# The order of small products in an RWKV-7 stage: three yields, a split solver, and sixteen gate pieces in the first group

## The chip, the cores and the metric

The kernel runs on one core of a Trainium2 chip. A core has five engines that run on their own and meet only at semaphores: TensorE (PE, matrix products; its weight loads are the row PEld), VectorE (DVE), ScalarE (ACT), GpSimd (POOL) and SyncE (SP, which here issues most of the DMA transfers). The metric is the device time of one execution in microseconds (us), and smaller is better.

## The reference, cut to what matters

The program is one layer of an encoder with four sequence mixers that share one projection, gates on their outputs, and a feed-forward network. The part that changes is the RWKV-7 mixer. Each of 8 heads keeps a 64 by 64 state S per direction, forward and backward over 1024 positions:

```python
S_t = S_{t-1} diag(w_t) + (S_{t-1} a_t) b_t^T + v_t k_t^T ;  y_t = S_t r_t
```

The other work in this stage belongs to the gates, `gates = sigmoid(u @ W_gate)`, which need nothing of the mixer and so can be computed at any moment:

```python
gates = jnp.split(jax.nn.sigmoid(p_gate), N_BRANCH, axis=-1)
merged = gates[0] * (ys[0] @ w_branch[l, 0])
for n in range(1, N_BRANCH):
    merged = merged + gates[n] * (ys[n] @ w_branch[l, n])
```

## The kernel before, in words

**Units.** The recurrence is done in chunks of 64 positions. A unit is one pair of heads (j of 0 to 3) and one block of 256 positions in each direction (bt of 0 to 3): 16 units, each with 4 chunks per direction. A unit passes through three generators. `rw_first` prepares it: `rw_dir` builds the operands `rw_AR` and `rw_BK` from decays (a scan on DVE, exponentials on ACT, products on DVE and POOL), then for each direction d eight products at L914 make the 64 by 64 coupling blocks, which DVE masks at L922 (four masks per d). When d = 1 is masked, `rw_solve` inverts the 16 by 16 diagonal blocks: eight DMAs bring the blocks to DRAM (`dA`, L967), two bring them back (`rw_SB`, `rw_pr`), ACT transposes one half (L973), DVE does a substitution in some 22 instructions (L981 to L994), two DMAs write the inverses out (`dT`, L997) and one reads them back in another layout (`rw_R`, L1000). `rw_second` assembles 64 by 64 inverses (`rw_TF`) from these in four pieces of 32 by 32 products (L1021, L1028, L1041, L1049). `rw_chain` then walks the four chunk steps of the unit.

**A chunk step of the chain.** L1112 multiplies the state by the operands (8 small products, called the step's first product below); ACT copies the result to `rw_s`; L1122 applies `rw_TF`, which gives u; ACT copies u into `rw_uv` (L1125); L1129 and L1136 form the new state in PSUM (L1136 reads u); DVE scales it into `rw_mv` for the next step (L1142; after the fourth step into `rw_M`). The outputs y are products at L1086 and L1091.

**Groups.** The loop in `rwkv` overlaps three units: in group g it runs the chain of unit g-1, the second part of unit g and the first part of unit g+1. One group has four steps, st = 0 to 3, which are the four chunk steps of the chain. Group 0 has no chain yet. Between these small products stand pieces of the gate work: one piece is 6 products of 128 by 512 (L125 to L127), 8 pieces make one column block of gates, and 28 column blocks (224 pieces) are spread over the stage. `GATE1` pieces run ahead of the groups, `GATE0` pieces in group 0, and `rate` says how many a step gets afterwards.

**What sets the order.** In the groups PE runs in exactly the order in which the Python code issues its instructions (`manual_schedule`). The queues of the other engines are ordered by the framework's scheduler, which starts from the same order and puts what is marked `high_priority` (the chain's own products, copies and state updates) further ahead. Each engine then works off its queue in order. The gates' weights come through `w_raw` (DMA by SP), `w_hi` (ACT) and `w_lo` (POOL), and a finished column block leaves PSUM through `gt` (ACT).

Of the kernel before, what the change touches and what calls it, by code (L numbers as in the profile page):

```python
# [23 lines left out]
class K:  # L24
# [661 lines left out]
    def rw_setup(self, wp):  # L686
        nc, a = self.nc, self.a
        self.rw_mask = self.t(wp, [P, 2, P], "rwm")
        self.rw_lm = self.t(wp, [P, 2, 32], "rwlm")
        self.rw_ST = self.t(wp, [64, 272], "rw_ST")  # L690
        nc.sync.dma_start(out=self.rw_ST[:, :256], in_=a["k_eye16"].to_broadcast([64, 256]))
        for tl, nm in ((self.rw_mask, "k_rwm"), (self.rw_lm, "k_rwl")):
            nc.sync.dma_start(out=tl, in_=a[nm])
        W = P * self.NB
        self.rw_rst = self.t(wp, [P, W], "rwrs", dt=BF16)
        nc.gpsimd.memset(self.rw_rst, 1.0)
        nc.gpsimd.memset(self.rw_rst[:, ::64], 0.0)

        NC = 2 * self.NB
        self.rw_TFt = [self.t(wp, [P, 2, NC, 64], f"rw_TF{i}") for i in range(2)]  # L700
        for x in self.rw_TFt:
            nc.gpsimd.memset(x, 0.0)
        self.rw_turn = 0
        self.rw_M = {}

        z = self.rw_TFt[0].rearrange("p d m t -> p (d m t)")
        for i in range(2):
            nc.sync.dma_start(out=self.dT[i].rearrange("g v x s t -> (g v x s t)").rearrange("(p n) -> p n", p=P),
                              in_=z[:, :256])
# [184 lines left out]
    def rw_first(self, j, bt, lin, wp):  # L894


        nc = self.nc
        NT, NB = T // P, self.NB
        NC = 2 * NB
        n0 = [bt * NB, NT - NB - bt * NB]  # L900
        cb = self.t(wp, [P, 2, NC, P], "rw_cb", bufs=3)
        gc = self.t(wp, [P, 2, NC], "rw_gc", bufs=3)
        ops = [self.rw_dir(j, d, n0[d], lin[d], gc[:, d], wp) for d in range(2)]
        b = dict(j=j, bt=bt, n0=n0, ar=[o[0] for o in ops], bk=[o[1] for o in ops], gc=gc, cb=cb, i=self.rw_turn)
        self.rw_turn += 1
        yield b
        for d in range(2):
            ar, bk, _ = ops[d]
            hrs = [(slice(64 * h, 64 * h + 64), slice(64 - 64 * h, P - 64 * h)) for h in range(2)]

            pts = [self.ps([P, NC, P], self.pat()) for h in range(2)]
            for c in range(NC):
                for h, (hr, _) in enumerate(hrs):
                    nc.tensor.matmul(pts[h][:, c, :], lhsT=bk[hr, c, :, :], rhs=ar[hr, c, :, h, :], start=True, stop=True)  # L914
            for h, (hr, ho) in enumerate(hrs):
                pt = pts[h]
                for o, rows, x in ((cb[hr, d], hr, pt[hr]),
                                   (ar[ho, :, :, h, :], ho, pt[ho].rearrange("p c (x t) -> p c x t", x=2))):
                    m = self.rw_mask[rows, d]
                    if len(o.shape) == 4:  # L920
                        m = m.rearrange("p (x t) -> p x t", x=2)
                    nc.vector.tensor_tensor(o, x, m.unsqueeze(1).to_broadcast(list(o.shape)), op=MUL)  # L922
            if d == 1:
                self.rw_solve(b, wp)
            yield
        pt = self.ps([P, 2, NB, 2], self.pat())
        for d in range(2):
            for n in range(NB):
                nc.tensor.matmul(pt[:, d, n, :], lhsT=ops[d][2][:, P * n:P * n + P], rhs=self.rw_sel[:, j, :],
                                 start=True, stop=True)  # L930
        for d in range(2):
            nc.scalar.copy(self.rw_coef[:, d, n0[d]:n0[d] + NB, 2 * j:2 * j + 2], pt[:, d])
        yield

    def rw_btm(self, b, wp):
# [19 lines left out]
    def rw_solve(self, b, wp):  # L955


        nc = self.nc
        NC = 2 * self.NB
        cb = b["cb"]  # L960
        rs = lambda q: slice(32 * q, 32 * q + 32)

        turn = b["i"] % 2
        dA = self.dA[turn].rearrange("(g u) (s t) -> u s g t", u=8, t=16)
        for u in range(8):
            o = 16 * (u % 4)
            nc.sync.dma_start(out=dA[u], in_=cb[16 * u:16 * u + 16, :, :, o:o + 16].rearrange("p d c t -> p (d c) t"))  # L967
        SB = self.t(wp, [64, 272], "rw_SB")
        pr = self.t(wp, [64, 256], "rw_pr")
        S1 = pr[:, :256].rearrange("p (s t) -> p s t", t=16)  # L970
        nc.sync.dma_start(out=SB[0:32, :256], in_=self.dA[turn, 0:32])
        nc.sync.dma_start(out=S1[32:64].rearrange("p s t -> p (s t)"), in_=self.dA[turn, 32:64])
        nc.scalar.copy(SB[32:64, :256].rearrange("p (s t) -> p s t", t=16), S1[32:64].rearrange("p s t -> p t s"))  # L973
        ST = self.rw_ST

        def view(x, w, o, n):

            return x.rearrange("p (x w) -> p x w", w=w)[:, :, o:o + 16 * n].rearrange("p x (i c) -> p x i c",
                                                                                     c=16)[:, :, :, :n]
        G = self.t(wp, [64, 64], "rw_G")  # L980
        nc.vector.tensor_copy(out=view(ST, 34, 1, 1), in_=view(SB, 34, 1, 1))  # L981
        for n in (2, 4, 8):
            x = 8 // n
            bij, tii, tjj, xij = [view(y, 34 * n, o, n) for y, o in ((SB, n), (ST, 0), (ST, 17 * n), (ST, n))]
            g3 = G[:, :x * n * n].rearrange("p (x i j) -> p x i j", x=x, i=n)
            m = min(n, 4)
            p4 = pr[:, :x * m * n * n].rearrange("p (x i j k) -> p x i j k", x=x, i=m, j=n)
            for l, r, o in ((bij, tjj, g3), (tii, g3, xij)):
                for i in range(0, n, m):
                    for y in range(x):  # L990
                        nc.vector.tensor_tensor(p4[:, y], l[:, y, i:i + m].unsqueeze(2).to_broadcast([64, m, n, n]),
                                                r[:, y].rearrange("p k j -> p j k").unsqueeze(1).to_broadcast(
                                                    [64, m, n, n]), op=MUL)
                    nc.vector.tensor_reduce(o[:, :, i:i + m], p4, axis=AX.X, op=ADD)  # L994

        for x in range(2):
            nc.sync.dma_start(out=self.dT[turn, :, :, x, :, 16 * x:16 * x + 16].rearrange("g v s t -> (g v) s t"),  # L997
                              in_=ST[x::2, :256].rearrange("p (s t) -> p s t", t=16))
        R = b["R"] = self.t(wp, [P, 2, NC, 32], "rw_R", bufs=2)
        nc.sync.dma_start(out=R.rearrange("p d m t -> p (d m) t"), in_=self.dT[turn].rearrange("g v x s t -> (v x s) g t"))  # L1000
# [56 lines left out]
    def rw_chain(self, b, wp):  # L1057


        nc = self.nc  # L1060
# [44 lines left out]
        for st in range(NC):  # L1105
# [24 lines left out]
                                     tile_position=(64 * h, 64 * h))  # L1130
            if st:
                y(st - 1, 0)
            with prio():
                for d, c in enumerate(cs):
                    for h, hr, _ in halves:
                        nc.tensor.matmul(pm[hr, d, :], lhsT=b["btm"][:, d, c, hr], rhs=b["uv"][:, d, c, h, :], start=False,  # L1136
                                         stop=True, tile_position=(0, 64 * h), skip_group_check=True)
                for h, hr, _ in halves:
                    g = b["gc"][hr, 0, st:st + 1]
# [119 lines left out]
    def rwkv(self, dr, dG, es, extra):  # L1259
        nc = self.nc  # L1260
# [40 lines left out]
        prev = None  # L1301

        with self.tc.manual_schedule(engines={mybir.EngineType.PE}):
            for g in range(n + 1):
                chn = self.rw_chain(prev, wp) if prev is not None else iter(())
                sec = self.rw_second(cur, wp) if cur is not None else iter(())
                fst, nxt = iter(()), None
                for st in range(4):
                    next(chn, None)
                    if st == 2:  # L1310
                        next(sec, None)
                    elif st == 3:
                        next(sec, None)
                        next(fst, None)
                    if prev is not None:
                        pieces(1)
                    next(chn, None)
                    if st == 0:
                        if cur is not None:
                            self.rw_btm(cur, wp)  # L1320
                        if g + 1 < n:
                            fst = self.rw_first(*order[g + 1], lin, wp)
                            nxt = next(fst)
                    elif st < 3:
                        next(fst, None)
                    if st > 1:
                        next(sec, None)
                    if st == 3 and g + 2 < n:
                        lin = self.rw_lin(*order[g + 2], wp)
                    if prev is None:  # L1330
                        pieces(self.GATE0 // 4)
                    else:
                        credit += rate if g < n else rate + self.ENDF / 2
                        k = int(credit + 1e-6)
                        credit -= k
                        pieces(k)
                next(chn, None)
                prev, cur = cur, nxt
            for _ in self.filler:
# [1 line left out]
        self.WP, self.wact = 300, False  # L1341

    HP = 300
    GATE0 = 8
    GATE1 = 8
    VA = 2
    NG = 28
# [751 lines left out]
```

## Time and profile before

| | |
|---|---|
| median of 3 runs | 2783.84 us (2767.37 to 2787.01) |
| the profiled execution, its own time | 2781.43 us |
| its span in the profile | 2779.6 us |
| PE busy | 2554.3 us, 92% |
| DVE, ACT, POOL busy | 64%, 33%, 43% |
| mean granted TensorE clock | 0.96 of full speed |

The profile names instructions by engine, line and operands: `L1136 MATMUL ppc<-rw_uv,rw_btm` writes a PSUM tile from the two tiles behind the arrow. "Idle before" is the time an engine stood still ahead of an instruction, and the name behind `<-` is what ended it. The granted clock (PEclk) is 1.00 at 2.4 GHz and 0.50 at 1.2 GHz; a value between is a mean over a stretch that has both. Times inside the span are counted from its start.

### The profile page before, as it was taken

The numbers are of one execution on the slowest core, as the hardware profiler recorded it, in microseconds if no ns is written. First come the engines' busy times: TensorE is split into PE (matmuls) and PEld (weight loads), VectorE is DVE, ScalarE is ACT, GpSimd is POOL, SyncE is SP. The second block draws the span as 40 slices with busy tenths as digits, with TensorE's granted clock in tenths as the row PEclk, the third lists the DMA queues.
The fourth block names the chain that finished last, engine by engine and source line by source line (L and its number), as shares of the span: only waits on it lengthen the run. The fifth ranks groups of instructions, "written<-read, shape, count | busy, mean of one in ns | idle before, by whom it ended". The sixth has DMA issues, their size and how long they took to land. (4 is left out here: it accounts for less than half of the span.)

```text
span 2779.6 us, 47056 instructions
## 1 busy us (share of the span) xinstructions
PE 2554.3 (92%) x18625; PEld 2044.3 (74%) x18625; DVE 1786.4 (64%) x2868; ACT 911.0 (33%) x1649; POOL 1194.1 (43%) x1164
## 2 busy tenths in 40 slices
PE   5999878999998899889989999999998999999998
PEld 4777656777776677678777777788776788888887
DVE  7577765676566642665562676457469998896444
ACT  4355532333333332333232232111234444442002
POOL 3654452343344323732222344357555444435332
PEclk9999988999999999999999979999999999999999
DMA  6422342443344323411111444455542222225222
GB/s 212 130 69 65 97 136 69 116 112 102 97 113 104 95 72 112 118 45 43 40 39 32 138 133 152 167 182 168 173 122 96 84 79 88 72 72 193 87 80 76
DMA packets 402117, 290.25 MB, mean 104 GB/s; under 512 B 121258, under 2 KB 364248, under 8 KB 401896
## 3 DMA queue, kind: packets, MB, share of 16 engines
q1 hardware_dynamic: 362920, 247.85, 30.6%
q10 hardware_dynamic: 38976, 39.40, 4.3%
q8 instruction: 146, 2.39, 0.4%
q14 instruction: 75, 0.61, 0.1%
HBM read 223.40 MB, written 63.77 MB: 103 GB/s over the span
## 5 line engine op out<-in xcount | busy, mean ns | idle before, releaser
L119 POOL TENSOR_TENSOR w_lo<-w_raw,w_hi 128x512 fp32r<-128x512 f32 x284 | 397.1, 1399 | 741.7 <-DVE w_hi L118 276.4
L125 PE MATMUL pbig<-uh,w_hi 128*128 128x512 f32 x1208 | 505.6, 420 | 20.5 <-ACT w_hi L116 8.9
L127 PE MATMUL pbig<-uh,w_lo 128*128 128x512 f32 x1208 | 483.4, 402 | 5.0 <-POOL w_lo L119 4.8
L126 PE MATMUL pbig<-ul,w_hi 128*128 128x512 f32 x1184 | 475.8, 402 | 0.0
L125 PEld LDWEIGHTS pbig<-uh,w_hi 128*128 128x128 f32 x1208 | 234.9, 195 | 86.8 <-ACT gt L1224 15.8
L127 PEld LDWEIGHTS pbig<-uh,w_lo 128*128 128x128 f32 x1208 | 232.9, 193 | 61.0 <-POOL w_lo L119 9.2
L126 PEld LDWEIGHTS pbig<-ul,w_hi 128*128 128x128 f32 x1184 | 230.2, 194 | 42.0 <-issue 0.9
L118 DVE CAST w_hi<-w_raw 128x512 fp32r<-128x512 f32 x224 | 136.4, 610 | 147.1 <-PE pbig L126 72.2
L127 PE MATMUL ppc<-uh,w_lo 128*128 128x512 f32 x340 | 134.1, 397 | 1.5 <-POOL w_lo L119 1.1
L125 PE MATMUL ppc<-uh,w_hi 128*128 128x512 f32 x340 | 134.2, 399 | 1.2 <-DVE w_hi L118 1.2
L126 PE MATMUL ppc<-ul,w_hi 128*128 128x512 f32 x320 | 126.6, 396 | 0.0
L125 PE MATMUL ppa<-uh,w_hi 128*128 128x512 f32 x220 | 88.5, 402 | 5.6 <-DVE w_hi L118 5.6
L127 PE MATMUL ppa<-uh,w_lo 128*128 128x512 f32 x220 | 87.0, 396 | 0.8 <-POOL w_lo L119 0.8
L127 PE MATMUL ppy<-uh,w_lo 128*128 128x512 f32 x216 | 85.1, 394 | 1.4 <-POOL w_lo L119 1.1
L125 PE MATMUL ppy<-uh,w_hi 128*128 128x512 f32 x216 | 85.3, 395 | 0.1
L1824 ACT CAST w_hi<-s 128x512 fp32r<-128x512 f32 x84 | 52.0, 619 | 97.8 <-PE pbig L126 23.7
L126 PE MATMUL ppa<-ul,w_hi 128*128 128x512 f32 x208 | 82.9, 399 | 0.0
L126 PE MATMUL ppy<-ul,w_hi 128*128 128x512 f32 x208 | 81.8, 393 | 0.0
L125 PEld LDWEIGHTS ppc<-uh,w_hi 128*128 128x128 f32 x340 | 64.9, 191 | 16.4 <-DVE w_hi L118 2.1
L127 PEld LDWEIGHTS ppc<-uh,w_lo 128*128 128x128 f32 x340 | 64.7, 191 | 16.4 <-POOL w_lo L119 1.5
L1375 DVE SCALAR_TENSOR_TENSOR ada_acc<-ada_w,sc,ada_acc 128x256 f32<-128x256 f32 x112 | 73.9, 662 | 2.0
L1142 DVE TENSOR_TENSOR rw_mv<-ppc,rw_gc 64x128 f32<-64x128 f32 x96 | 27.7, 289 | 73.5 <-PE ppc L1136 71.5
(789 smaller groups left out, 6361.9 us busy)
## 6 DMA issues: line engine op xcount, KB each, us to landing
w_raw<-in_w_in_dram SPq DMA_DIRECT2D x172, 256.0 KB
ada_w<-in_ada_w_dram SPq DMA_DIRECT2D x24, 1024.0 KB
s_raw<-in_ffn_up_dram SPq DMA_DIRECT2D x84, 256.0 KB
dG<-gt ACTq DMA_DIRECT2D x64, 256.0 KB
sgt<-dG SPq DMA_DIRECT2D x32, 512.0 KB
rw_in<-dIn SPq DMA_DIRECT2D x32, 384.0 KB
w_raw<-in_ffn_down_dram SPq DMA_DIRECT2D x44, 256.0 KB
dF<-cv SPq DMA_DIRECT2D x22, 512.0 KB
```

The lines of the kernel that those rows point to most:

```text
L118: nc.vector.tensor_copy(out=hi, in_=raw[:, k0:k0 + m])
L119: nc.gpsimd.tensor_tensor(lo, raw[:, k0:k0 + m], hi.bitcast(F32), op=SUB)
L125: nc.tensor.matmul(pt, lhsT=wh, rhs=uh, start=start, stop=False)
L126: nc.tensor.matmul(pt, lhsT=wh, rhs=ul, start=False, stop=False)
L127: nc.tensor.matmul(pt, lhsT=wl, rhs=uh, start=False, stop=stop)
L1142: nc.vector.tensor_tensor(mo, pm[hr], g, op=MUL)
L1375: nc.vector.scalar_tensor_tensor(acc, w[:, k, :], self.sc[:, k:k + 1], acc, op0=MUL, op1=ADD)
L1824: nc.scalar.copy(hi, x)
```

## The change

`rw_solve` becomes a generator: its first part issues the DMAs to and from `dA`, its second part the copy on ACT, the substitution and the DMAs of `dT` and `rw_R`. `rw_first` runs the first part where it ran the whole before, and the second part in a step of its own, which the loop takes at the end of the group. `rw_chain` gets a third yield per step, between the copy of u with the products that don't need it and the products at L1136 that do; what the loop issues at that point (the transposes `rw_btm` in st 0, the products of d = 0 and d = 1 in st 1 and st 2, the bonus coefficients L929 in st 3) now stands ahead of L1136. `rw_lin` (L839) moves to the end of the group. `GATE0` is 16 in place of 8, and every step of group 0 too has a piece at its head; with the same 224 pieces in all, `rate` falls from 2.125 to 2.0 pieces per step. The helper `issue_after(ins)` orders, behind the instruction it is given, those instructions of its block that are on the same engine; it is given a product on PE, and the block holds instructions of ACT, DVE and SP.

```diff
@@ rw_first
             if d == 1:
-                self.rw_solve(b, wp)
+                solve = self.rw_solve(b, wp)
+                next(solve)
             yield
...
             nc.scalar.copy(self.rw_coef[:, d, n0[d]:n0[d] + NB, 2 * j:2 * j + 2], pt[:, d])
+        yield
+        next(solve, None)
         yield
@@ rw_solve
         nc.sync.dma_start(out=S1[32:64].rearrange("p s t -> p (s t)"), in_=self.dA[turn, 32:64])
+        yield
         nc.scalar.copy(SB[32:64, :256].rearrange("p (s t) -> p s t", t=16), S1[32:64].rearrange("p s t -> p t s"))
@@ rw_chain
             if st:
                 y(st - 1, 0)
+            yield
             with prio():
                 for d, c in enumerate(cs):
                     for h, hr, _ in halves:
-                        nc.tensor.matmul(pm[hr, d, :], lhsT=b["btm"][:, d, c, hr], rhs=b["uv"][:, d, c, h, :], start=False,
+                        self.last_pm = nc.tensor.matmul(pm[hr, d, :], lhsT=b["btm"][:, d, c, hr], rhs=b["uv"][:, d, c, h, :], start=False,
@@ rwkv
                 for st in range(4):
                     next(chn, None)
-                    if st == 2:
+                    if st > 1:
                         next(sec, None)
-                    elif st == 3:
-                        next(sec, None)
-                        next(fst, None)
-                    if prev is not None:
-                        pieces(1)
+                    pieces(1)
                     next(chn, None)
                     if st == 0:
...
-                    elif st < 3:
+                    else:
                         next(fst, None)
+                    next(chn, None)
                     if st > 1:
                         next(sec, None)
-                    if st == 3 and g + 2 < n:
-                        lin = self.rw_lin(*order[g + 2], wp)
                     if prev is None:
-                        pieces(self.GATE0 // 4)
+                        pieces(self.GATE0 // 4 - 1)
                     else:
                         credit += rate if g < n else rate + self.ENDF / 2
...
                         pieces(k)
+                    if st == 3:
+                        if g + 2 < n:
+                            lin = self.rw_lin(*order[g + 2], wp)
+                        with self.tc.issue_after(self.last_pm.ins) if self.last_pm is not None else ExitStack():
+                            next(fst, None)
-    GATE0 = 8
+    GATE0 = 16
```

PE, step st 1 of one group in the middle of the stage, before (L1122 makes u, L1136 reads its copy, L914 are the products of d = 0):

```order
L1122 MATMUL ppc_9857<-rw_s_9837,rw_TF_190_720 64x64 x4
L1129 MATMUL ppc_9864<-rw_mv_9217,ident_73 64x128 x2
L1086 MATMUL ppy_9867<-rw_uv_9212,rw_cb_8696 64x64 x2
L1091 MATMUL ppy_9867<-rw_mv_9217,rw_AR_8705 64x64 x2
L1091 MATMUL ppy_9867<-rw_mv_9217,rw_AR_8730 64x64 x2
L1136 MATMUL ppc_9864<-rw_uv_9212,rw_btm_9222 64x64 x4
L1086 MATMUL ppy_9867<-rw_uv_9212,rw_cb_8696 64x64 x2
L914 MATMUL ppt_9882<-rw_AR_9769,rw_BK_9770 128x128
...
L125 MATMUL pbig_9824<-uh_13_83,w_hi_9547 128x512
```

The same place in the changed kernel (its lines are numbered up to 6 higher: L1127 is L1122, L1142 is L1136, L915 is L914):

```order
L1127 MATMUL ppc_9869<-rw_s_9861,rw_TF_190_720 64x64 x4
L1134 MATMUL ppc_9876<-rw_mv_9229,ident_73 64x128 x2
L1091 MATMUL ppy_9879<-rw_uv_9224,rw_cb_8716 64x64 x2
L1096 MATMUL ppy_9879<-rw_mv_9229,rw_AR_8725 64x64 x2
L1096 MATMUL ppy_9879<-rw_mv_9229,rw_AR_8750 64x64 x2
L915 MATMUL ppt_9886<-rw_AR_9783,rw_BK_9784 128x128
...
L1142 MATMUL ppc_9876<-rw_uv_9224,rw_btm_9234 64x64 x4
L1091 MATMUL ppy_9879<-rw_uv_9224,rw_cb_8716 64x64 x2
L125 MATMUL pbig_9733<-uh_15_85,w_hi_9391 128x512
```

The eight products of d = 0 now stand between u and the state; the state products follow them and have only two output products and the gate pieces behind them.

ACT, step st 3 of a group, before (`rw_s` and `rw_uv` are the chain's copies, `rw_SB` is the solver's, which waits for its DMA):

```order
L1115 COPY rw_s_6350<-ppc_6345 128x128
L932 COPY rw_coef_707<-ppa_6371 128x2x2 x2
L1224 ACTIVATE gt_6384<-pbig_6081 128x512
L116 CAST w_hi_6482<-w_raw_6480 128x512
L973 COPY rw_SB_6262<-rw_pr_6263 32x256
L1224 ACTIVATE gt_6387<-pbig_6082 128x512
L1225 DMA dG_155_677<-gt_6384 128x512
L1125 COPY rw_uv_5475<-ppc_6390 64x2x64 x2
```

The same group in the changed kernel:

```order
L1120 COPY rw_s_6375<-ppc_6370 128x128
L1130 COPY rw_uv_5513<-ppc_6402 64x2x64 x2
L978 COPY rw_SB_6309<-rw_pr_6310 32x256
L934 COPY rw_coef_707<-ppa_6419 128x2x2 x2
L1105 COPY rw_ysb_6016<-ppy_6412 128x2x2x64
L1160 DMA dYr_705<-rw_ysb_6016 64x4x64 x3
L116 CAST w_hi_6657<-w_raw_6655 128x512
```

The copy of u now comes ahead of the solver's copy.

DVE, steps st 0 and st 1 of a group, before (`rw_mv` are the state updates of st 0 and st 1, `rw_RT` is the transpose that waits for the DMA of `rw_R`, L922 masks the products of d = 0):

```order
L876 TENSOR_TENSOR rw_AR_7124<-rw_in_7117,rw_l_1147_7007 64x4x63
L878 TENSOR_TENSOR rw_AR_7124<-rw_in_7117,rw_l_1147_7007 64x4x64
L1142 TENSOR_TENSOR rw_mv_6547<-ppc_7058,rw_gc_6018 64x2x64 x2
L884 SCALAR_TENSOR_TENSOR rw_BK_7100<-rw_tmp_7108,rw_tmp_7095 64x4x64 x2
L882 SCALAR_TENSOR_TENSOR rw_tmp_7133<-rw_l_1148_7009,rw_in_7117 128x256
L884 SCALAR_TENSOR_TENSOR rw_BK_7125<-rw_tmp_7133,rw_tmp_7120 64x4x64 x2
L1016 STREAM_TRANSPOSE rw_RT_7239<-rw_R_6843 128x256
L1142 TENSOR_TENSOR rw_mv_6547<-ppc_7188,rw_gc_6018 64x2x64 x2
L922 TENSOR_TENSOR rw_cb_7090<-ppa_7206,rwm_711 64x512
L922 TENSOR_TENSOR rw_AR_7099<-ppa_7206,rwm_711 64x8x64
```

The same group in the changed kernel (L1148 is L1142, L1021 is L1016, L923 is L922):

```order
L1148 TENSOR_TENSOR rw_mv_6579<-ppc_7102,rw_gc_6068 64x2x64 x2
L885 SCALAR_TENSOR_TENSOR rw_BK_7138<-rw_tmp_7146,rw_tmp_7133 64x4x64 x2
L877 TENSOR_TENSOR rw_AR_7162<-rw_in_7155,rw_l_1155_7038 64x4x63
...
L883 SCALAR_TENSOR_TENSOR rw_tmp_7171<-rw_l_1156_7040,rw_in_7155 128x256
L885 SCALAR_TENSOR_TENSOR rw_BK_7163<-rw_tmp_7171,rw_tmp_7158 64x4x64 x2
L1021 STREAM_TRANSPOSE rw_RT_7289<-rw_R_7071 128x256
L923 TENSOR_TENSOR rw_cb_7128<-ppa_7234,rwm_711 64x512
L923 TENSOR_TENSOR rw_AR_7137<-ppa_7234,rwm_711 64x8x64
...
L1148 TENSOR_TENSOR rw_mv_6579<-ppc_7224,rw_gc_6068 64x2x64 x2
```

Half of the `rw_AR` products moved behind the update of st 0, and the four masks of d = 0 moved ahead of the update of st 1. The substitution itself (L981 to L994, now L986 to L999) starts in both kernels right behind the copy `rw_E` of L1044 and ahead of the update of `rw_M` after st 3; in the changed kernel no `rw_AR` product stands among its instructions any more in the groups with a chain.

## Rows read from the trace of the kernel before

**Rows 1.** The page: engine's busy time and share; granted clock in 40 slices.

```profile
PE 2554.3 (92%) x18625; PEld 2044.3 (74%) x18625; DVE 1786.4 (64%) x2868; ACT 911.0 (33%) x1649; POOL 1194.1 (43%) x1164
PEclk9999988999999999999999979999999999999999
```

**Rows 2.** Windows: stretch, length, busy per engine, PEclk, DMA; group 0, 15 groups, last.

```profile
391.00:441.60 50.60, 28.55 (x303) 22.90 (x300) 34.60 (x84) 12.88 (x31) 18.16 (x24) 0.73 0.25 65
441.60:1046.00 604.40, 552.02 (x7427) 427.94 (x7426) 381.09 (x957) 200.56 (x543) 231.99 (x350) 0.95 0.38 99
1046.00:1080.00 34.00, 33.83 (x279) 25.73 (x279) 2.74 (x9) 7.80 (x21) 5.14 (x4) 1.00 0.23 66
```

**Rows 3.** Waits of PE in the 15 groups: total, times, longest.

```profile
PE ppc L1136 <- ACT rw_uv L1125: 34.6, 27, 4.3
PE ppc L1112 <- DVE rw_mv L1142: 10.8, 10, 2.9
```

**Rows 4.** Timeline, ACT (first two) and PE in st 3: start, length, instruction, idle before.

```profile
758.62 0.62 ACT L973 COPY rw_SB<-rw_pr 32x256 f32<-32x256 f32 x1 [2.08 <-DMA rw_pr<-dA]
759.27 0.54 ACT L1125 COPY rw_uv<-ppc 64x128 f32<-64x128 f32 x2
759.58 0.73 PE L1136 MATMUL ppc<-rw_uv,rw_btm 128*64 128x64 f32 x8 [1.21 <-ACT rw_uv L1125]
```

**Rows 5.** Windows: steps st 0 to st 3 of the group that starts at 728.1.

```profile
728.10:736.40 8.30, 7.16 (x57) 5.31 (x56) 7.88 (x17) 4.54 (x12) 6.04 (x10) 1.00 0.54 135
736.40:744.10 7.70, 7.70 (x79) 6.01 (x78) 4.35 (x9) 1.41 (x4) 5.28 (x7) 1.00 0.59 179
744.10:753.20 9.10, 9.10 (x207) 7.32 (x206) 4.40 (x10) 1.50 (x5) 0.51 (x1) 1.00 0.16 37
753.20:766.90 13.70, 12.19 (x166) 9.47 (x165) 7.37 (x31) 7.32 (x21) 5.09 (x11) 1.00 0.44 109
```

**Rows 6.** Timeline of PE: two gate products in a row, at either clock.

```profile
724.47 0.63 PE L126 MATMUL pbig<-ul,w_hi 128*128 128x512 f32 x1
724.90 0.63 PE L127 MATMUL pbig<-uh,w_lo 128*128 128x512 f32 x1
728.86 0.39 PE L126 MATMUL pbig<-ul,w_hi 128*128 128x512 f32 x1
729.09 0.40 PE L127 MATMUL pbig<-uh,w_lo 128*128 128x512 f32 x1
```

**Rows 7.** Windows: the clock around the end of one group's st 3.

```profile
719.80:726.60 6.80, 6.80 (x72) 5.75 (x69) 6.39 (x23) 2.05 (x5) 2.49 (x8) 0.51 0.37 83
726.60:740.20 13.60, 12.46 (x113) 9.31 (x113) 10.76 (x23) 5.33 (x15) 10.85 (x14) 0.99 0.54 144
```

**Rows 8.** Waits of PE in group 0.

```profile
PE pps L1021 <- DVE rw_RT L1016: 10.1, 1, 10.1
PE pps L1049 <- DVE rw_E L1044: 5.0, 1, 5.0
```

**Rows 9.** Timeline of DVE: first and last of one substitution; first mask of d = 1.

```profile
718.86 0.17 DVE L981 COPY rw_ST<-rw_SB 64x8 f32<-64x8 f32 x1 [5.28 <-ACT rw_SB L973]
729.02 0.41 DVE L994 TENSOR_REDUCE rw_ST<-rw_pr 64x32 f32<-64x256 f32 x1
749.70 0.68 DVE L922 TENSOR_TENSOR rw_cb<-ppa,rwm 64x512 f32<-64x512 f32 x1 [0.74 <-PE ppt L914]
```

**Rows 10.** Timeline of DVE in the group that starts at 845.6.

```profile
857.73 0.41 DVE L994 TENSOR_REDUCE rw_ST<-rw_pr 64x32 f32<-64x256 f32 x1
...
865.45 0.45 DVE L1016 STREAM_TRANSPOSE rw_RT<-rw_R 128x256 f32<-128x256 f32 x1 [3.50 <-DMA rw_R<-dT]
865.93 0.68 DVE L922 TENSOR_TENSOR rw_cb<-ppt,rwm 64x512 f32<-64x512 f32 x1
```

**Rows 11.** Waits of DVE in the 15 groups.

```profile
DVE rw_RT L1016 <- DMA rw_R<-dT: 26.9, 7, 5.8
```

**Rows 12.** Waits of SP's queue in the 15 groups.

```profile
SPq L997 <- DVE rw_ST L994: 36.2, 11, 5.3
```

More of the change, by code (lines that the diff above doesn't have):

```diff
@@ L706, in rw_setup @@
         z = self.rw_TFt[0].rearrange("p d m t -> p (d m t)")
+        self.last_pm = None
         for i in range(2):
```

## The prediction, written before the changed kernel was run

> **What bounds the kernel now.** I began with the page's table of engines: PE is busy for 92% of the span, and no other engine comes near [rows 1]. Time can therefore leave this kernel in two ways only: PE waits less, or PE does its work at a higher clock. The change touches one stage, so next I cut the trace into windows. Group 0 takes 50.6 us at a clock of 0.73, the 15 groups with a chain 604.4 us (40.3 each) with PE busy for 552.0 at 0.95, and the last one 34.0 us with PE busy throughout [rows 2]. The waits of PE in the 15 groups show two of size: 34.6 us for `rw_uv`, the copy of u, and 10.8 us for `rw_mv`, the state update [rows 3]. The timeline tells why the first is late in st 3: on ACT the solver's copy `rw_SB` stands ahead of it, waits 2.08 us for its DMA, and the copy of u follows within 0.03 us of its end; PE stands 1.21 us [rows 4]. The windows of that group's four steps show that PE has idle time in st 0 and st 3 alone [rows 5].
>
> **A, the waits for u.** After the change ACT copies u ahead of `rw_SB`, and 2 to 8 small products stand between L1122 and L1136 (the transposes L952 in st 0, the masked blocks' products in st 1 and 2, L929 in st 3). The first takes away the late copy of st 3, the second covers the copy itself. Of the 34.6 us [rows 3] I keep 0.17 us a group, by choice, for copies that end just behind their cover: 2.6 us. A is -32; if only half of it is cover, -17. `rw_SB` waits behind `rw_uv` now, but loses at most the copy's 0.54 us [rows 4].
>
> **B, the gate pieces.** `rate` falls by 0.125 in each of four steps, half a piece per group. A piece is 6 products, which follow each other by 0.23 us at full clock (0.43 at half) [rows 6]: 15 x 0.5 x 6 x 0.23 = 10.3 us leave the groups (5 if the pieces were covering waits that stay). They go to group 0, which gets 8 pieces more, 48 products. About 24 of them stand ahead of L1021, where PE waits 10.1 us for `rw_RT` [rows 8]; at half clock they take 24 x 0.43 = 10.3 us and fill that wait. The 24 behind it cost 5.5 us at full and 10.3 at half clock, less the 5.0 us that PE waits at L1049 [rows 8], since the copy `rw_E` no longer stands behind a substitution. Group 0: 0.5 to 5.3 longer, I take +3.
>
> **C, the solver's loop.** This is the step that I cannot read off a row. In the changed kernel DVE has `rw_RT`, which waits for the DMA of `rw_R`, and four masks of d = 0 ahead of the state update of st 1; in the trace that update came first. Whatever holds `rw_R` now holds the chain. When is it there? The first mask of d = 1 began at 749.70, 5.6 us into st 2 [rows 5, 9]; as L1136 and the outputs move behind the masked products, I take 4.9. From that mask to the end of `rw_SB` passed 759.24 - 749.70 = 9.5 us [rows 4, 9], the substitution took from 718.86 to 729.43, 10.5 us [rows 9], and from its end to the start of `rw_RT` passed 865.45 - 858.14 = 7.3 us [rows 10]: 27.3 us in all. So `rw_R` comes 32.2 us after the start of st 2. Steps st 2 and st 3 will take 9.1 and, with one wait of 1.21 us and some clock given back, about 10.8 [rows 5]; this puts it at 12.3 us after the next st 0. The update of st 1 has to be done when st 2 wants it, 8.3 + 7.7 us after that start [rows 5]; transpose (0.45), four masks (4 x 0.68) and the update (0.6, a figure by the copy of u, 0.54) take 3.8 off this, so `rw_R` must be there at 12.2 [rows 4, 9, 10]. Just late, then: 1 us of stall a group, +15. The bounds: nothing (it comes earlier), and 7.6 us in all 15 groups, +114, by the lateness told under the third rival. The 10.8 us for `rw_mv` [rows 3] stay: fewer pieces stand behind L1136 but no less than two.
>
> Of the moved step's DMAs: in the trace SP's queue stood ready for the writes of `dT` in 11 groups and waited for the substitution's result, 36.2 us in all [rows 12]. The queue thus adds nothing, and in the new order the writes stand behind the same loads of `rw_mv` and one load of `w_raw`. `rw_lin` moves behind two pieces; its activations and DVE work lie beside gate products, and what they would delay, the `rw_AR` of st 0, has moved behind the state update of st 0 as well. DVE is the engine without slack there (7.88 of 8.30 us busy [rows 5]), and delay on it is in C's upper bound. The void order on `issue_after` costs nothing: the substitution stands where it stood, behind `rw_E`.
>
> **D, the clock.** At 0.95 the 15 groups lose 604.4 x 0.05 = 30 us [rows 2]. The drop comes with st 3: the window at the end of one st 3 shows 0.51, the next again 0.99 [rows 7], and it follows the stretch of small products and the wait for u. If that wait goes, half the loss may: -14, between 0 and -28.
>
> **The sum.** -32 - 10.3 + 3 + 15 - 14 = -38.3 on the profiled 2781.4 gives 2743.1. The median of the runs is 2.4 higher, so I say 2745. A group would take (604.4 - 41.3) / 15 = 37.5 us. With the bounds of A to D apart from C's far one (I take 40 for it), this case spans 2715 to 2785.
>
> **Rivals.** *More comes back.* `rw_R` is never late and the stage runs to its loop: 27.3 from first mask to `rw_RT`, 3.8 for masks and update, 4.9 to the next mask, 36.0 us a group. 15 x (40.3 - 36.0) = 64 less, group 0 +3: 2723. For it: `rw_RT` waits only 26.9 us in 7 of the groups now [rows 11]. Against it: the other waits would all have to vanish too. Chance 0.12.
>
> *Given back.* The time won for u goes to `rw_RT` on DVE and from there to `rw_mv`: a stall of 2 us a group, +30, and no clock: -32 - 10.3 + 3 + 30 = -9.3, 2775. For it: the shorter the group, the later `rw_R` is in it, as the 27.3 us do not shrink. Chance 0.18.
>
> *Slower.* The head of DVE's queue. In the group of 845.6 `rw_RT` began 19.8 us after st 0 [rows 10], 7.6 past the 12.2 that C allows; there the update stood ahead, so PE hardly felt it. If 10 of 15 groups are like this, 76 us stand against A, B and group 0's 39.3: +36.7, 2821. It decides the sign from 5.2 such groups on, and passes 1% from 9. For it: `rw_RT` waited in 7 groups, up to 5.8 us [rows 11]. Against it: substitutions that late came where other DVE work stood among their instructions, and in the new order none does. Chance 0.11. The Trainium skill, page "TensorE: Matmul & The Clock Gate", section "Architectural detail: the array is 16× 32×32, not 1× 128×128", says that ACT and DVE are strict FIFO; by it no update can pass a transpose that waits, and the stall reaches PE whole. The trace agrees, as the copy of u began only when `rw_SB` had ended [rows 4].
>
> *It doesn't do what it says.* If the tie did hold the substitution until the last state products, it would start some 1 us later in a group and the 27.3 would be 28.3: +15 on the forecast, 2760. The order shows no such tie, chance 0.01.
>
> **Numbers.** The forecast has 0.58. About 1% is what a measurement of this kernel can tell: faster means below 2756.0, slower above 2811.7. Faster: 0.12 and some 0.47 of the forecast's 0.58, 0.59. Slower: 0.11. Within 1%: the rest, 0.30. The range takes in the better case down to 2714 and giving back up to 2792, which leaves out the slower case and little of the others.
>
> **What would show it.** A: the waits of PE at the state products for `rw_uv` come to 3 or 4 us. B: group 0's wait for `rw_RT` is under 2 us and that at L1049 gone. C: DVE's waits for `rw_R` stand ahead of st 1's update, and PE's waits for `rw_mv` come to about 25 us. D: the 15 groups' clock is near 0.97. All of it: a group takes 37.5 us. I am wrong if groups still take 40 us, or if PE waits over 40 us for `rw_mv`; then the DVE queue has taken what ACT's gave.

## The result, and the profile after

The changed kernel takes 2741.6 us (median of 4 runs, 2736.6 to 2752.2) against 2783.5 for the kernel before: a ratio of 0.986, 95% interval 0.983 to 0.988. A second set of runs gave 2745.0 and 0.986 (0.983 to 0.988). Forecast were 2745 and a range of 2714 to 2792. The time came out as predicted; two of the steps behind it did not: the path of step C, and the price of nothing for the move of `rw_lin`.

The profiled execution is the slowest of its four, 2752.2 us. The page's row of PE and of the granted clock, as in [rows 1]:

```profile
PE 2539.7 (92%) x18625; PEld 2032.3 (74%) x18625; DVE 1781.4 (65%) x2868; ACT 916.3 (33%) x1653; POOL 1178.2 (43%) x1164
PEclk9999998999999999999989988999999999999999
```

The windows of group 0, the 15 groups with a chain and the last group (columns as in [rows 2]):

```profile
390.60:440.60 50.00, 34.05 (x356) 27.01 (x354) 31.62 (x76) 14.13 (x31) 18.33 (x23) 0.86 0.30 77
440.60:1016.50 575.90, 531.30 (x7385) 409.24 (x7384) 387.24 (x966) 199.73 (x544) 217.32 (x351) 0.97 0.41 103
1016.50:1050.50 34.00, 33.78 (x276) 25.20 (x276) 3.39 (x11) 7.84 (x21) 6.72 (x7) 1.00 0.23 67
```

The 15 groups shrank by 28.5 us to 38.4 each, and group 0 ended 1.0 earlier: 29.5 us in this stage. PE's idle time in the groups fell from 52.4 to 44.6, its busy time by 20.7 (fewer gate products, and a higher clock). Behind the start of the last group nothing moved in this pair of profiles (1733.6 us before, 1733.9 after), so the stage accounts for 30 of the some 40 us between the medians. In the thirteen profiles told of here besides that of the kernel before, this one among them, that stretch scatters from 1723.9 to 1737.3 us with no tie to an edit that I can see; the other 10 us stay unexplained.

PE's waits in the 15 groups, against [rows 3] (us in total, times, longest):

```profile
PE ppc L1117 <- DVE rw_mv L1148: 28.7, 17, 3.1
PE pbig L125 <- ACT gt L1230: 5.9, 5, 2.8
PE ppc L1142 <- ACT rw_uv L1130: 5.6, 2, 3.2
PE ppa L956 <- ACT rw_l L844: 3.6, 5, 0.7
```

The wait for u is nearly gone (34.6 to 5.6) and that for the state update grew from 10.8 to 28.7. The timeline of ACT in a step st 3 shows the first, against [rows 4]: the copy of u waits only for PE, and the solver's copy comes after it.

```profile
707.06 0.54 ACT L1130 COPY rw_uv<-ppc 64x128 f32<-64x128 f32 x2 [1.89 <-PE ppc L1127]
708.64 0.62 ACT L978 COPY rw_SB<-rw_pr 32x256 f32<-32x256 f32 x1 [1.03 <-DMA rw_pr<-dA]
```

The windows of st 0 to st 3 of the group at 673.8, against [rows 5], show where time is now lost: st 3 is 10.1 us without a gap, and PE's idle time is in st 0.

```profile
673.80:685.00 11.20, 7.37 (x56) 5.17 (x55) 10.51 (x23) 5.25 (x14) 5.06 (x9) 1.00 0.51 121
685.00:694.50 9.50, 9.50 (x78) 7.10 (x78) 8.18 (x17) 1.86 (x6) 7.29 (x10) 0.82 0.45 126
694.50:704.20 9.70, 9.66 (x207) 7.11 (x206) 4.51 (x10) 3.67 (x10) 1.29 (x1) 1.00 0.27 76
704.20:714.30 10.10, 10.10 (x159) 8.38 (x158) 4.88 (x25) 3.63 (x11) 1.51 (x7) 1.00 0.44 109
```

The timelines of PE and of DVE in that st 0 say why. PE starts the state products at 678.46; the update that scales them runs at 684.62, because DVE first ends the substitution (L999) and makes four `rw_AR`:

```profile
678.46 0.45 PE L1142 MATMUL ppc<-rw_uv,rw_btm 128*64 128x64 f32 x8
...
684.95 0.77 PE L1117 MATMUL ppc<-rw_mv,rw_AR 128*64 128x64 f32 x8 [3.05 <-DVE rw_mv L1148]
```

```profile
679.98 0.41 DVE L999 TENSOR_REDUCE rw_ST<-rw_pr 64x32 f32<-64x256 f32 x1
680.32 0.67 DVE L863 TENSOR_TENSOR_SCAN rw_tmp<-rwrs,rw_l 128x256 f32<-128x256 bf16 x1
...
682.47 0.85 DVE L877 TENSOR_TENSOR rw_AR<-rw_in,rw_l 64x252 f32<-64x252 f32 x1
683.25 0.61 DVE L879 TENSOR_TENSOR rw_AR<-rw_in,rw_l 64x256 f32<-64x256 f32 x1
683.89 0.69 DVE L863 TENSOR_TENSOR_SCAN rw_tmp<-rwrs,rw_l 128x256 f32<-128x256 bf16 x1
684.62 0.61 DVE L1148 TENSOR_TENSOR rw_mv<-ppc,rw_gc 64x128 f32<-64x128 f32 x2
...
688.89 0.44 DVE L1021 STREAM_TRANSPOSE rw_RT<-rw_R 128x256 f32<-128x256 f32 x1
```

DVE has no gap longer than 0.17 us in this stretch, and `rw_RT` waits for nothing. In the 15 groups it waits for `rw_R` once, in the last of them, and DVE's largest wait is for the solver's blocks (against [rows 11]):

```profile
DVE rw_ST L986 <- ACT rw_SB L978: 58.2, 14, 5.7
...
DVE rw_RT L1021 <- DMA rw_R<-dT: 5.0, 1, 5.0
```

### The profile page after: what moved, and what is told of

Read it like the earlier page. It is cut to its first block, busy times and chain, and to the rows that moved or that the text cites. A ratio compares the mean times of both kernels' runs of the same rounds, so it can differ in the third digit from the quotient of the medians.

```text
span 2750.4 us, 46997 instructions
## 1 busy us (share of the span) xinstructions
PE 2539.7 (92%) x18625; PEld 2032.3 (74%) x18625; DVE 1781.4 (65%) x2868; ACT 916.3 (33%) x1653; POOL 1178.2 (43%) x1164
## 5 line engine op out<-in xcount | busy, mean ns | idle before, releaser
L127 PEld LDWEIGHTS pbig<-uh,w_lo 128*128 128x128 f32 x1208 | 233.4, 194 | 62.0 <-POOL w_lo L119 10.8
L127 PEld LDWEIGHTS ppc<-uh,w_lo 128*128 128x128 f32 x340 | 65.8, 194 | 17.9 <-POOL w_lo L119 2.6
L204 ACT CAST uh<-h_raw 128x1024 fp32r<-128x1024 f32 x22 | 23.0, 1052 | 151.9 <-PE ppc L127 123.8
```

Source lines behind the costliest of these rows:

```text
L127: nc.tensor.matmul(pt, lhsT=wl, rhs=uh, start=False, stop=stop)
L204: nc.scalar.copy(hi, src)
```

## The experiments

Each was timed beside the kernel before on the same chip; the sets ran on different chips, so kernels of different sets compare by their ratios. Ratios are to the kernel before; "u" and "mv" are PE's waits for `rw_uv` and `rw_mv` in the 15 groups.

| kernel | median us | ratio (95%) | 15 groups, us | u | mv | clock |
|---|---|---|---|---|---|---|
| before | 2783.5 to 2786.1 | 1 | 604.4 | 34.6 | 10.8 | 0.95 |
| changed, again | 2745.0 | 0.986 (0.983, 0.988) | 576.2 | 4.9 | 28.8 | 0.97 |
| e2_whole | 2746.3 | 0.986 (0.983, 0.989) | 572.5 | 6.2 | 28.0 | 0.98 |
| e3_noyield | 2763.5 | 0.991 (0.989, 0.994) | 589.2 | 28.1 | 8.8 | 0.95 |
| e4_split | 2782.1 | 0.999 (0.997, 1.001) | 608.2 | 34.2 | 11.6 | 0.94 |
| e6_linback | 2790.0 | 1.002 (1.000, 1.004) | 612.5 | 0.6 | 50.4 | 0.94 |
| e10_lin_only | 2770.2 | 0.995 (0.993, 0.997) | 599.0 | 40.4 | 2.6 | 0.95 |
| e1_gate0_8 | 2757.3 | 0.990 (0.988, 0.993) | 585.9 | 9.2 | 18.4 | 0.97 |
| e5_gate0_24 | 2762.2 | 0.992 (0.989, 0.994) | 583.5 | 13.7 | 20.4 | 0.95 |
| e7_late12 | 2772.1 | 0.995 (0.993, 0.997) | 605.9 | 14.8 | 25.3 | 0.93 |
| e8_updfirst | 2757.7 | 0.990 (0.987, 0.993) | 589.6 | under 1.2 | 3.4 | 0.94 |
| e9_tie_d1 | 2748.3 | 0.987 (0.985, 0.990) | 577.2 | 4.4 | 31.2 | 0.98 |
| e11_tf_act | 2727.1 | 0.979 (0.977, 0.981) | 550.5 | 4.2 | 12.4 | 0.99 |

**Once more, as it is.** 

> The changed kernel once more, as it is, beside the two that follow: 2738 to 2752 with a profile like the first one's (waits for rw_mv 25 to 32 us, for rw_uv 4 to 8 us).

All of it held.

### Which part took the waits for u away

**e2_whole**: the solver in one piece.

```diff
-                next(solve)
+                for _ in solve:
+                    pass
             yield
```

> The changed kernel with the solver in one piece again (its second part issued right behind its first, where the masks of d = 1 are); the third yield, rw_lin at the end and 16 gate pieces stay. Theory 1, from the order of the instructions: the third yield alone puts the copy of u ahead of rw_SB on ACT, and the split adds nothing; PE's waits at the state products for rw_uv stay near 6 us in the 15 groups, the time stays within 8 us of 2741.6. Theory 2, the reading that the split puts the solver's copy behind u: the waits for rw_uv return to 25 us or more and the time rises to 2765 to 2775.

**e4_split**: the kernel before, with the split and nothing else.

```diff
-                self.rw_solve(b, wp)
+                solve = self.rw_solve(b, wp)
+                next(solve)
             yield
...
                         pieces(k)
+                    if st == 3:
+                        next(fst, None)
```

> The kernel before with the split solver alone, its second part issued at the end of st 3. Theory 1: neither ACT's nor DVE's queue is changed around it, so the waits for rw_uv stay near 34.6 us and the time within 8 us of 2783. Theory 2 (the split is what moved the u copy ahead): waits for rw_uv under 10 us and the time 2745 to 2760.

**e3_noyield**: the changed kernel without the third yield.

```diff
                 y(st - 1, 0)
-            yield
             with prio():
...
-                    next(chn, None)
                     if st > 1:
```

> The changed kernel without the third yield: the state products L1142 directly behind the copy of u, as before the change; the split solver, rw_lin at the end and 16 gate pieces stay. Theory 1 (the yield is what takes the u waits away): waits for rw_uv come back to 25 to 35 us, the waits for rw_mv fall from 28.7 towards the 10.8 us of before, and the time is 2755 to 2775. Theory 2 (the split does it): waits for rw_uv stay below 10 us, those for rw_mv fall, and the time is 2720 to 2735.

Theory 1 held three times. Without the split the time and both waits stay; the split alone moves nothing; without the yield the wait for u is back, and in ACT's timeline of e3_noyield the old pair stands again:

```profile
594.59 0.62 ACT L978 COPY rw_SB<-rw_pr 32x256 f32<-32x256 f32 x1 [4.14 <-DMA rw_pr<-dA]
595.24 0.55 ACT L1130 COPY rw_uv<-ppc 64x128 f32<-64x128 f32 x2
```

So the third yield is what takes the copy of u ahead on ACT, by what the scheduler makes of the new order; how much the products that it puts between L1127 and L1142 add as cover was not separated. The helper around the split's second part has no effect: the program built without it has the same instructions in the same order on every engine.

### The move that I costed at nothing

**e6_linback**: the changed kernel with `rw_lin` where it was.

```diff
+                    if st == 3 and g + 2 < n:
+                        lin = self.rw_lin(*order[g + 2], wp)
                     if prev is None:
...
-                        if g + 2 < n:
-                            lin = self.rw_lin(*order[g + 2], wp)
```

> The changed kernel with rw_lin back ahead of the last pieces of st 3. The prediction costed this move at nothing: 2736 to 2748. The rival: with rw_lin earlier its scans and products stand between the substitution's instructions on DVE again (in the order of this kernel or by its timing), the substitution ends later and rw_R with it; then 2755 or more, with DVE waiting over 20 us for rw_R.

**e10_lin_only**: the kernel before with that move alone.

```diff
-                    if st == 3 and g + 2 < n:
-                        lin = self.rw_lin(*order[g + 2], wp)
                     if prev is None:
...
                         pieces(k)
+                    if st == 3 and g + 2 < n:
+                        lin = self.rw_lin(*order[g + 2], wp)
```

> The kernel before with rw_lin moved to the end of the group, and nothing else: ACT still copies u behind rw_SB, and there are 8 gate pieces in group 0. If the move is good by itself, as taking it back cost 40 us or more, the substitution stands together on DVE and DVE's waits for rw_R fall from 26.9 to under 10 us; the waits for rw_uv (34.6 us) stay. In the kernel before, the update of st 1 stood ahead of rw_RT, and PE lost nearly nothing to rw_R; so the time moves little: 2770 to 2788. The rival, that the move gains its 40 us without the third yield too: 2735 to 2755.

Taken back, this move costs the whole gain: 2790.0. The waits for u stay away (0.6), but those for `rw_mv` reach 50.4. Two views of e6_linback, PE's and DVE's waits in its 15 groups (the DVE row from its own table):

```profile
PE ppc L1117 <- DVE rw_mv L1148: 50.4, 14, 5.5
```

```profile
DVE rw_RT L1021 <- DMA rw_R<-dT: 34.5, 10, 5.6
```

Its DVE timeline, in the st 0 that begins at 647.4, shows the mechanism: DVE's queue now has the `rw_AR` products among the last steps of the substitution (L996, L999), and the update stands behind all of them. That the scheduler does so because the decays are ready earlier is my reading; no run shows it by itself.

```profile
652.03 0.95 DVE L877 TENSOR_TENSOR rw_AR<-rw_in,rw_l 64x252 f32<-64x252 f32 x1
...
655.55 0.40 DVE L999 TENSOR_REDUCE rw_ST<-rw_pr 64x32 f32<-64x256 f32 x1
...
657.30 0.96 DVE L879 TENSOR_TENSOR rw_AR<-rw_in,rw_l 64x256 f32<-64x256 f32 x1
658.29 0.64 DVE L996 TENSOR_TENSOR rw_pr<-rw_ST,rw_G 64x256 f32<-64x256 f32 x1
...
659.73 0.41 DVE L999 TENSOR_REDUCE rw_ST<-rw_pr 64x32 f32<-64x256 f32 x1
660.18 0.61 DVE L1148 TENSOR_TENSOR rw_mv<-ppc,rw_gc 64x128 f32<-64x128 f32 x2
```

The update is 13 us into the group here, against 10.8 in the changed kernel's group shown above. Over all 15 groups it starts 11.4 us into the group in the mean, against 9.2, and ten of the substitutions have all eight `rw_AR` products among their steps and take 15.1 to 18.0 us; in the changed kernel none has any, and they take 9.8 to 10.9. Alone, the move gives 14 us (2784.6 to 2770.2 in that set; its profiled execution, the slowest of its seven, shows 7 of them up to the end of the 15 groups); the rest of the change without it costs 4 (2785.7 to 2790.0); both together give 40. The update of st 0 stands behind all eight `rw_AR` products in 14 of the 15 groups there, and in one of 15 in the changed kernel: in this way DVE gives back what the yield gains on ACT.

### Where the new wait sits

**e7_late12**: in st 1 and st 2 the products of d = 0 and d = 1 go behind the state products again.

```diff
-                    else:
+                    elif st == 3:
                         next(fst, None)
 
                     next(chn, None)
+                    if st in (1, 2):
+                        next(fst, None)
```

> The changed kernel with the coupling products of d = 0 and d = 1 behind the state products again in st 1 and st 2; the third yield then has something between its halves in st 0 and st 3 only. On DVE the update of st 1 then stands ahead of the four masks, but the update of st 0 behind all eight rw_AR products. My predicted step C (the masks and rw_RT in front of st 1's update hold the chain): the waits for rw_mv fall from 28.7 to about 12 us and the time to 2715 to 2730. The rival, from the trace after the change (the wait is at the update of st 0, behind DVE's own preparation): the 1 us waits in st 1 go, about 9 us in 9 groups, but the waits in st 0 stay or grow by the 2 us of the further rw_AR products; rw_mv 25 to 45 us, time 2735 to 2765.

It got worse than either theory said: 2772.1. No wait was left at the update of st 1, but mv fell by 3 us only, all ten of its waits standing at the update of st 0; u rose to 14.8, and the clock fell to 0.93. The path of step C is thus not what holds the chain for most of the 28.7 us; why the clock and ACT suffered was not pursued.

**e8_updfirst**: `rw_dir` of the next unit is ordered behind the update of st 0 on DVE.

```diff
+                    self.last_mv = nc.vector.tensor_tensor(mo, pm[hr], g, op=MUL)
...
+                    if st == 0 and g + 1 < n:
+                        with self.tc.issue_after(self.last_mv.ins) if self.last_mv is not None else ExitStack():
+                            fst = self.rw_first(*order[g + 1], lin, wp)
+                            nxt = next(fst)
```

> The changed kernel with rw_dir's work of the next unit (scans, rw_AR, rw_BK) ordered on DVE behind the state update of st 0, by the same helper but given that update, an instruction of DVE. If the update of st 0 is late because it stands behind DVE's own preparation, the waits for rw_mv in st 0 (about 20 of 28.7 us) go; in return the preparation starts when the update is done, about as early as now, and the products of d = 0 in st 1 may wait up to 2 us for rw_BK in each group. Expected: waits for rw_mv about 10 us, the granted clock of the 15 groups 0.99, time 2715 to 2735. If rw_R and the masks in st 1 bound the chain (my predicted step C), the wait only moves to st 1: rw_mv stays at 25 us or more, time 2738 to 2755.

The wait for `rw_mv` went to 3.4 us, and none of it is left at the update of st 0, which shows its cause. The time did not follow: PE's table of e8_updfirst has the wait at the products of d = 0 instead, for operands that POOL makes from what DVE now makes later. I had allowed 2 us a group for this and it took 1.7. PE's idle time in the groups still fell by 5.1 us against the changed kernel (44.6 to 39.5); its busy time rose by 18.8 with the same products, at a clock of 0.94, and that ate the gain.

```profile
PE ppa L916 <- POOL rw_BK L891: 13.5, 14, 2.0
PE ppt L916 <- POOL rw_BK L891: 11.8, 14, 2.0
...
PE ppc L1118 <- DVE rw_mv L1149: 3.4, 3, 1.1
```

**e9_tie_d1**: only `rw_dir` of d = 1 is held so (a yield between the two calls of `rw_dir`, and the `issue_after` above around the second).

> The changed kernel with only the second half of rw_dir (d = 1: scan, rw_AR, rw_BK) ordered on DVE behind the state update of st 0; d = 0 stays free, so that POOL's rw_BK of d = 0, which PE waited for by 25.3 us when both halves were held, comes as early as now. Where the update of st 0 waits behind all eight rw_AR products, it comes 2.3 us earlier, which is about half of the groups: the waits for rw_mv fall from 28.7 to 12 to 20 us, the waits for rw_BK stay below 6 us, and the time is 2725 to 2738. If the loop through the solver bounds the groups whatever stands ahead of the update, the wait reappears at rw_BK or at the update of st 1: 2742 to 2760.

The second case: 2748.3, mv 31.2 in 22 waits, which now stand at the update of st 1 as often as at that of st 0. Both times that DVE's work was only put in another order, it gave its time back at the next place.

**e11_tf_act**: work is taken off DVE; the copies L1057 go to ACT.

```diff
-            nc.vector.tensor_copy(out=TF[rs(q0), d, :, 32 * (q1 % 2):32 * (q1 % 2) + 32], in_=pe[rs(q0)])
+            nc.scalar.copy(TF[rs(q0), d, :, 32 * (q1 % 2):32 * (q1 % 2) + 32], pe[rs(q0)])
```

> The changed kernel with the four copies of rw_TF (L1057, 1.24 us of DVE per group, standing among the substitution's instructions) on ACT. If what bounds a group now is the work on DVE from the start of the substitution to the update of st 0 and the masks, the substitution ends 1.2 us earlier: 15 x 1.24 = 19 us less, the waits for rw_mv fall from 28.7 to 10 to 20 us, the time is 2718 to 2735. If the bound is the round trip of the blocks by DMA or PE itself, DVE only waits longer and the time is 2740 to 2750. If ACT, which copies u in the same stretch, is in the way: waits for rw_uv or rw_s above 15 us and 2750 or more.

The first case: 2727.1 us, ratio 0.979 (0.977 to 0.981), faster than both kernels (the changed one had 0.983 to 0.988). The window of its 15 groups and PE's first wait in them:

```profile
438.20:988.70 550.50, 523.79 (x7385) 403.47 (x7384) 365.00 (x903) 216.04 (x604) 220.00 (x351) 0.99 0.42 108
```

```profile
PE ppc L1117 <- DVE rw_mv L1148: 12.4, 14, 1.7
```

For 22 us of DVE's busy time (387.2 to 365.0) the groups gave 25.4. Of these 16.3 are the wait for `rw_mv`; PE's busy time fell by 7.5 with the same products, at a clock of 0.99. The medians differ by less, 14 to 18 us; the profiled execution is the fastest of its five here, and that of the changed kernel the slowest of its four. A group takes 36.7 us, near the 36.0 that the prediction had as the loop's floor.

### The gate pieces

**e1_gate0_8** and **e5_gate0_24**: 8 and 24 pieces in group 0.

```diff
-    GATE0 = 16
+    GATE0 = 8
```

> The changed kernel with 8 gate pieces in group 0 in place of 16, so 2.125 pieces per step afterwards. By the predicted step B the 15 groups grow by 15 x 0.5 x 6 x 0.23 = 10.3 us of PE work; by the trace after the change group 0 was no longer with 16 pieces than with 8, so it gives back 0 to 1. Expected: 2750 to 2753. The rival, that these products only fill waits for rw_mv in the groups: 2738 to 2745, with the waits for rw_mv falling from 28.7 to about 18 us. If the clock in group 0 hangs on the pieces, its granted clock falls from 0.87 to about 0.73 and its length stays near 50 us.

> The changed kernel with 24 gate pieces in group 0 (5 at the end of each step), 1.875 pieces per step afterwards. Group 0 still waits 11.9 us for rw_RT, and about 4 of the 8 new pieces (5.5 us) stand ahead of that wait. If the groups go on losing PE work one for one: -10.3 in the groups, up to +5.5 in group 0, 2735 to 2740. If the groups have come to DVE's loop (the trace of the change has DVE busy or waiting for the solver's DMA all round), the missing products turn into waits for rw_mv: 28.7 grows to 35 to 39 us, and the time is 2742 to 2750.

With 8, the 15 groups take 10 us more, as B had it, and group 0 ends earlier (at 433.9, its clock at 0.80 and not 0.73); the median is 12 to 16 us above the changed kernel, a little more than I expected. From the copy `rw_SB` near the start of group 0 (390.62 here, 391.96 in the changed kernel) to the first product of the chain pass 43.3 us with 8 pieces and 48.7 with 16; before the change, with 8 pieces, it was 49.9. So the eight pieces cost group 0 5.4 us, and the rest of the change took 6.6 off it. With 24 both of my cases were too low: PE has 48 products less in the groups, yet they take 583.5 us. The window of e5_gate0_24 shows the clock at 0.95 with PE's busy time hardly lower:

```profile
443.90:1027.40 583.50, 529.04 (x7337) 408.69 (x7336) 381.02 (x956) 195.88 (x539) 213.96 (x349) 0.95 0.39 100
```

So taking pieces out of the groups helped from 8 to 16 in group 0; with 24 there, new waits in the groups (u 13.7, and 12.0 for `rw_BK`) and the lower clock cost more than the products did. Where the better number lies between was not tried.

## Why the prediction was right, and where it was not

**A, right.** -32 was forecast, and 29.0 us of waits for u went. The copy of u did come ahead of `rw_SB`. I read this off the order of the whole change, which has the split solver and the yield in it, and did not say which of them does it; e2_whole and e4_split show that the split has no part in it, and e3_noyield that the yield has nearly all. How much of the 29.0 is the order on ACT and how much the cover, the other half of the step, stays open.

**B, right in the groups, too small in group 0.** 10.3 was forecast; e1_gate0_8 puts it at 10 in the groups. For group 0 I took +3, and against e1_gate0_8 it is +5.4, the upper end of what I had allowed; in the pair of before and after it is hidden, as the rest of the change shortened group 0 by more (it ended 1.0 earlier). The wait for `rw_RT` was not filled, which was a sign that I had named: it is 11.9 us, where I had put it under 2. The step that failed there is the half clock that I took for the pieces ahead of it: from that copy `rw_SB` PE reaches the wait after 17.9 us with 46 gate products at a clock of 1.00, against 19.6 with 24 at 0.74 before, and 16.7 with 22 at 0.80 in e1_gate0_8, which takes back only the pieces. The row of group 0, against [rows 8]; the wait at L1049 is gone, as predicted:

```profile
PE pps L1026 <- DVE rw_RT L1021: 11.9, 1, 11.9
```

**C, wrong in mechanism, right in size by luck.** +15 was forecast and the wait for `rw_mv` grew by 17.9. My working had `rw_R` late by 0.1 us (12.3 against 12.2); the 1 us a group was a choice. The step that failed is "Whatever holds `rw_R` now holds the chain". The transpose did come 13 to 15 us after st 0 in most groups, past my limit of 12.2, but it did not wait: `rw_R` had landed, and DVE came to it late. Of the 28.7 us, 23.6 are at the update of st 0, behind DVE's own work, and the rest, some 1 us in five groups (5.1 in all), at that of st 1, the place that I had named. e8_updfirst removes it by order and e11_tf_act most of it by taking work away. Even e6_linback, where DVE does wait 34.5 us for `rw_R`, has all but 2.8 us of its 50.4 at the update of st 0.

**`rw_lin`, wrong.** The words "lie beside gate products" were said of a move that decides the sign of the change. I had the evidence in hand without the link: the third rival named substitutions with other DVE work among their instructions, and the order showed that this was gone, but I did not ask which part of the change had done it. e6_linback is near to that rival, at 2790 where the rival had 2821, but through the `rw_AR` products ahead of the update of st 0 rather than through `rw_R`.

**D, right in size.** 604.4 x 0.05 = 30 us were lost to the clock before, 575.9 x 0.03 = 17 after: -13 for -14 forecast. The step had the drop follow the wait for u. The windows of st 0 and st 1 above show that it now follows the wait of 3.05 us for `rw_mv`: 1.00 in st 0, 0.82 in st 1. In the clock's record of this trace the clock falls in ten places of the 15 groups: seven stand at or right behind a wait for `rw_mv`, two at one for `rw_uv` and one at one for `gt`; before the change, seven of eleven stood at waits for `rw_uv`. So the places moved with the waits and are hardly fewer; the time at the lower level fell from 58 to 34 us. Over the kernels of the table, with the waits for u, mv and `rw_BK` added up, the mean clock is 0.99 at 17 us, 0.97 or 0.98 at 30 to 36, and 0.93 to 0.95 at 37 to 51; e8_updfirst, with 0.94 at 29, is the exception, and there eleven of thirteen falls come right behind its waits for `rw_BK`. This goes together; it doesn't show which is the cause. No experiment changed the clock alone.

**The sum.** In the groups -41.3 was forecast and -28.5 came: A gave 3.0 less, C cost 2.9 more, waits for `rw_l` (3.6) and more for `gt` (1.5) were not in my sum, a wait of 1.9 for `rw_RT` in the groups went, and PE's busy time fell by 20.7 where B and D had 24.3. The median met the forecast to 3 us, but that is luck in part: some 10 us of the difference between the medians lie outside the stage, which neither the change nor my sum touches. The upper end of my span, 2785, is also too low by its own rule: it takes C's 40 and no gain of the clock, but A and B at their middle values; with -17, -5 and +5.3 for these the sum is 2807.

## What to carry to other kernels

Where a scheduler orders the in-order engines, a move of one producer (here `rw_lin`) can change what stands in the queue of another far more than the edit that one is looking at: undo each part of a change by itself before giving it the credit. When a wait moves from ACT to DVE, look whether DVE waits for something or is just busy ahead of it: here two changes of DVE's order gave nothing, and 1.2 us per group moved from it to an engine with slack shortened the groups by 25 us and the median by 14 to 18. Shortening the solver's trip through DRAM, for which DVE waits 58.2 us, was not tried. Filler taken out of this loop helped only until the loop's next waits were uncovered.

## What the runs showed of the hardware that was not expected

The same `rw_AR` product on DVE (L879, both operands in SBUF) takes 0.42 us in the 13 cases of the changed kernel's 15 groups with POOL idle. Of the 43 beside work of POOL, 21 take 0.41 or 0.42 us and 22 take 0.61 or 0.94 to 0.95. Each of the 22 ends 0.27 or 0.28 us after the end of the POOL instruction that ran when it began. In the timeline of DVE above, the one at 683.25 took 0.61 and ended at 683.86; POOL's instruction L860 beside it ended at 683.59:

```profile
681.41 0.79 POOL L887 TENSOR_SCALAR rw_l<-rw_l,rw_kah,rw_omka 128x256 f32<-128x256 f32 x1 [5.79 <-DVE rw_tmp L883]
682.28 0.77 POOL L888 TENSOR_TENSOR rw_l<-rw_l,rw_in 128x256 f32<-128x256 f32 x1
683.02 0.57 POOL L860 TENSOR_SCALAR rw_l<-rw_l 128x256 f32<-128x256 f32 x1
```

The Trainium skill, page "SBUF — State Buffer", section "SBUF: two separate sides", says that DVE operations with two SBUF inputs and POOL operations that read SBUF exclude each other for a whole instruction. The lengths above agree: the 22 end as if they could begin only when POOL's instruction was done. In four of the other 21, L887 of POOL spans the whole product and is itself drawn out, to 0.95 to 1.41 us, where the one at 681.41 has 0.79. So moving DVE's products to POOL, which was not tried, might not free as much as it moves.

SP needs 4.94 us to issue the eight transfers to `dA`, more than half of the 8.5 us from there (700.15) to `rw_SB` (708.64 in ACT's rows above), and DVE waits 58.2 us for `rw_SB` in the groups. Whether two queues would shorten it was not tried. SP's timeline in st 2 of the group at 673.8:

```profile
700.15 4.94 SPq L971 DMA_DIRECT2D dA<-rw_cb  x8
```
